# Reordering the second half of an input projection: two reused weight groups first, compression under the convolution groups

## The chip, the cores and the metric

The kernel runs on one core of one Trainium2 chip. The metric is the device time of one launch in microseconds (us), lower is better.

## What is computed

One decoder layer on x of 2048 tokens by 1024 channels. The input projection gives 2328 columns: queries of 8 heads, three key/value pairs of 2 groups (compressed, selected, window), gates, and the input of a gated depthwise convolution over time of 512 channels and 31 taps. Then come sparse attention in blocks of 128 queries, a layer norm and SiLU over the convolution, an output projection over both, and a feed-forward network.

```
xn = rms_norm(x); proj = xn @ w_in                      # 1024 -> 2328
q, kc_raw, vc_raw, ks, vs, kw, vw, gates, conv_in = split(proj)
k_cmp, v_cmp = compress(kc_raw), compress(vc_raw)       # silu(blocks of 32 tokens @ w1) @ w2
o_nsa  = g0*softmax(q k_cmp) v_cmp + g1*softmax(q k_sel) v_sel + g2*softmax(q k_win) v_win
o_conv = silu(layer_norm(depthwise_conv(a * sigmoid(gate))))
x = x + concat(rms_norm(o_nsa), rms_norm(o_conv)) @ w_out
y = x + (silu(h @ w_gate) * (h @ w_up)) @ w_down,  h = rms_norm(x)
```

## The kernel before, in words

Every product of full precision is three matmuls of halves: weights and activations are split in a high and a low float16 part, and `mm3` (L244) issues high by high, high by low and low by high.

**Phase A** (`phase_A_body`, L360) is the input projection, in two halves of 1024 tokens, s = 0 and s = 1. A half has two blocks of 512 tokens, h = 0 and 1. The 1024 rows of w_in are used in nine column parts: parts 0 to 3 are the convolution's (a channel block and its gate, 256 columns), part 4 the raw compressed keys and values (`kcvc`), parts 5 to 8 the row groups, whose result has tokens on partitions: part 5 at column 768 of the kept row (values and gates), 6 at column 0, 7 at 256, 8 at 512. The list `seq` (L416) names the order in which parts are loaded (`loads`), normed (only for s = 0) and split (`casts`: ScalarE rounds the high half, L466, VectorE makes the low half, L467). The split weights wh and wl have 3 buffers each.

- A convolution part (`conv`, L476) is four products of 24 matmuls of 512 columns (`colmm`); ScalarE puts tanh of the gate into `sg` (one buffer) and the channel into `hc`, VectorE multiplies them (L488).
- The depthwise filter of a channel block is 50 VectorE steps on 512-wide tiles (`filters`, L318 to L353, with the running sums ev, fq and od), called taps. They are put into a list, and `mm3` takes one from it each time 2232 matmul columns have been issued (`PACE`, L50). What is left at the end of a half is issued there in one go (`while self.taps`, L601).
- `conv_tail` (L610) finishes 128 tokens of the convolution: four transposes on TensorE, then layer norm and SiLU in five VectorE and four ScalarE instructions, and a store to DRAM (`mixc`). The tile z has 2 buffers, the tile zt one. The eight tails of s = 0 are called during the first convolution part of s = 1. The eight tails of s = 1 come in phase B, at a priority a little under the attention's.
- A row step (`rows`, L507) is 24 matmuls for 128 tokens, a copy by ScalarE and a store.

In s = 1 a generator `ahead()` is pumped between the products: first `compress` (L639), 16 chunks of weights that ScalarE and POOL split (L235, L236) and of blocks that POOL splits too (L665), with 12 matmuls each; then `early_B` (L761), which prepares the first two query blocks: `prep0` and `prep0q` (rms norm, rope and transposes of q), `value_scales` (L740; the largest value is spread over the partitions by two small TensorE steps, L191 and L196, with a VectorE reduction between them, L193), and `prep1` (L944 to L983, the compressed attention of the block). In the kernel before, the pump gives two steps at each break of convolution parts 2 and 3 and one for each row step.

**Phase B** goes over 16 query blocks: `attend` (L1066 on: scores L1084 to L1089, exponentials L1094, value products L1117), and `project` (L1184 on: the output projection of two blocks' tokens, with its weights split at L242 and L243 before the first). The pool that holds the project's tiles (and the closing tile `zo` of each attention block, L1172) lies in the memory of phase A's long-lived pool, so the first of them waits until the last conv tail is done. Then the feed-forward network runs from about 1430 us on.

**The order.** Within phase A, TensorE's instructions stand as they are written (a manual schedule, L533). All other engines, and TensorE in phase B, get their order from a list scheduler by priorities; taps have a priority 3000 lower than the rest. Each engine runs its instructions in the order so fixed.

Of the kernel before, what the change touches and what calls it, by code (L numbers as in the profile page):

```python
# [94 lines left out]
class Body:  # L95
    def __init__(self, tc, I, out, phases="ABC"):
        self.tc, self.nc, self.I, self.out = tc, tc.nc, I, out
        with ExitStack() as ctx:
            self.c = ctx.enter_context(tc.tile_pool(name="const", bufs=1))
            self.dr = ctx.enter_context(tc.tile_pool(name="dram", bufs=1, space=DRAM))  # L100
            self.taps, self.credit = [], 0
            self.consts()
            pb = ctx.enter_context(ExitStack())
            with ExitStack() as pa:
                self.sa = pa.enter_context(tc.tile_pool(name="sbA1", bufs=1, side="right"))
                tails = self.phase_A(pb)
                self.open_B(pb)
                with tc.high_priority(-TAILP):
                    for t in tails:
                        self.conv_tail(*t)  # L110
            pc = ctx.enter_context(ExitStack())
            self.open_project(pc)
            last = self.phase_B()
            pb.close()
            self.ffn(last, pc.close)
            self.end()
# [243 lines left out]
    def phase_A_body(self, pb, ctx, ctx0):  # L360
# [52 lines left out]
                  ([(768, 896), (1024, 1152)], 512)]  # L413
        parts = [[(1816 + j * 128, 1944 + j * 128), (1304 + j * 128, 1432 + j * 128)] for j in range(4)]
        parts += [[(512, 768)]] + [g[0] for g in groups]
        seq = [(s, at) for s in range(2) for at in (0, 1, 4, 2, 3, 5, 6, 7, 8)]  # L416
        raws, sums, cast = [], [], []

        def loads(to):
# [50 lines left out]
        def take(t):  # L470
            loads(t + 2)
            norms(t + 1)
            casts(t)
            return cast[t]

        def conv(j, x2, w2, between):  # L476
            hc = sa.tile([128, 2, 512 + HALF], F32, name="hc", tag="hc", bufs=HCB)
            nc.vector.tensor_copy(hc[:, :, :HALF], halo[:, j])
            for h in range(2):
                p = colmm(0, x2[h], w2)  # L480
                between(2 * h)
                t = s0.tile([128, 2, 256], F32, name="sg", tag="sg", bufs=1)
                nc.scalar.activation(t, p.rearrange("p (m e) -> p e m", e=2), AF.Tanh, scale=w2[3])
                p = colmm(128, x2[h], w2)
                between(2 * h + 1)
                hv = hc[:, :, HALF + h * 256:HALF + (h + 1) * 256]
                nc.scalar.activation(hv, p.rearrange("p (m e) -> p e m", e=2), AF.Copy, scale=w2[2])
                nc.vector.scalar_tensor_tensor(hv, t, 1.0, hv, op0=ALU.add, op1=ALU.mult)  # L488
            nc.vector.tensor_copy(halo[:, j], hc[:, :, 512:])
            acc = sa.tile([128, 1024], F32, name="acc", tag="acc", bufs=4)  # L490
            self.taps += self.filters(hc, acc, j)
            return acc
# [40 lines left out]
        with tc.manual_schedule(engines={mybir.EngineType.PE}):  # L533
# [6 lines left out]
            for s in range(2):  # L540
# [10 lines left out]
                accs = []  # L551
                nxt = ahead() if s else iter(())
                pump = lambda: next(nxt, None)
                for j in range(4):
                    at = 9 * s + j + (j > 1)
                    w2 = take(at)

                    def between(i):
                        if i == 1:
                            casts(at + 1)  # L560
                        if j == 0 and i < 2:
                            step(st1, 4)
                        else:
                            for t in tails[:2 if j == 0 else 1]:
                                self.conv_tail(*tails.pop(0))
                            for _ in range(PUMP[j]):
                                pump()
                    accs.append(conv(j, x2, w2, between))
                    if j == 1:
                        next(gains, None)  # L570
                        kcvc(s, x2, take(at + 1), lambda: casts(at + 2))
                    if j == 2 and s == 0:
# [1 line left out]
                        next(out_scale)  # L574
                self.pace = PACE[2 * s + 1]
                for gi in range(2):
                    t = 9 * s + 5 + gi
                    wg = take(t), groups[gi][1]
                    for h in range(2):
                        rows(s, h, x2, wg, pump)  # L580
# [1 line left out]
                            casts(t + 1)  # L582
                        if s == 0 and gi == 1:
                            next(out_scale)
                norms(9 * s + 8)
                wg = [(take(9 * s + 5 + gi), groups[gi][1]) for gi in (2, 3)]
                for g in wg:
                    rows(s, 0, x2, g, pump)
                casts(9 * s + 9)
                if s == 0:  # L590
                    first, st0 = turn(load(1, 0))
                    rows(s, 1, x2, wg[0], lambda: step(st0, STEP0))
                    xs = load(1, 1)
                    rows(s, 1, x2, wg[1], nothing)
                    second, st1 = turn(xs)
                else:
                    for g in wg:
                        rows(s, 1, x2, g, pump)
                    for _ in nxt:
                        pass  # L600
                while self.taps:  # L601
# [158 lines left out]

    def early_B(self):  # L761
        self.sp = {c: self.prep0(c) for c in range(NE)}
        for _ in range(4):
            yield
        scales = self.value_scales()
        for _ in range(EW - 4):
            next(scales, None)
            yield
        for c in range(NE):
            self.prep0q(self.sp[c])  # L770
# [960 lines left out]
```

## Time and profile before

| what | value |
|---|---|
| median of 3 runs | 2785.3 us (2785.23 to 2785.98) |
| the profiled execution | 2789.21 us |
| its span in the profile | 2787.4 us, mean granted TensorE clock 0.958 |
| TensorE matmul, busy | 2495.3 us, 90% |
| VectorE, busy | 2182.1 us, 78% |
| ScalarE, busy | 1508.9 us, 54% |
| POOL, busy | 1319.8 us, 47% |
| second half of phase A | 244 to 554 us |
| phase B before the feed-forward network | 554 to about 1430 us |

Times inside the program count from the start of the span. An engine's idle time costs something only where another engine ends up waiting for it on the way to the end. The table is an average over the program: the feed-forward network, the last half, is nearly all TensorE, whereas in the stretch that the change touches VectorE and TensorE are about equally full.

### The profile page before, as it was taken

How to read it: one execution, taken by the hardware profiler on the slowest of the kernel's cores; microseconds unless marked ns; L12 is line 12 of the kernel's file. 1: busy time of each engine (PE TensorE's matmuls, PEld its weight loads, DVE VectorE, ACT ScalarE, POOL GpSimd, SP SyncE). 2: the span in 40 equal slices, each digit the busy share in tenths (PEclk: the TensorE clock that was granted, in tenths of full speed). 3: DMA queues.
4: the chain of work that ended last, by engine and by line, in shares of the span. 5: the costliest groups of instructions: out<-in, count | busy, mean ns of one | idle time of the engine just before them, and what ended most of it. 6: DMA issues, size and time to landing. Idle time of an engine off the chain costs nothing. (4 is left out here: it accounts for less than half of the span.)

```text
span 2787.4 us, 46922 instructions
## 1 busy us (share of the span) xinstructions
PE 2495.3 (90%) x17430; PEld 1522.7 (55%) x17430; DVE 2182.1 (78%) x3463; ACT 1508.9 (54%) x3153; POOL 1319.8 (47%) x1117
## 2 busy tenths in 40 slices
PE   6997977867889998889986999998899999899999
PEld 3485446745667777777873444443344444344444
DVE  4898898889999899889666766668766765797995
ACT  7534633477666666555564555555455444445543
POOL 1101345254444444334455665667666664951850
PEclk9998988878999999999997999999999999999999
DMA  6133212113211111000015433443344332677343
GB/s 216 55 111 104 85 52 63 56 48 114 74 57 42 45 47 36 28 28 28 28 43 187 139 105 105 133 136 113 118 136 136 116 100 106 212 243 260 105 148 110
DMA packets 254781, 283.33 MB, mean 102 GB/s; under 512 B 20304, under 2 KB 174344, under 8 KB 254552
## 3 DMA queue, kind: packets, MB, share of 16 engines
q1 hardware_dynamic: 253904, 278.93, 31.2%
q8 instruction: 136, 2.23, 0.3%
q0 software_dynamic: 400, 1.31, 0.1%
q14 instruction: 93, 0.76, 0.1%
q10 hardware_dynamic: 248, 0.09, 0.0%
HBM read 201.96 MB, written 78.32 MB: 101 GB/s over the span
## 5 line engine op out<-in xcount | busy, mean ns | idle before, releaser
L1394 PE MATMUL ps<-oph,wh 128*128 128x512 f16 x1232 | 470.8, 382 | 30.1 <-DVE u L1472 12.7
L1397 PE MATMUL ps<-opl,wh 128*128 128x512 f16 x1232 | 470.1, 382 | 2.8 <-POOL opl L1353 1.3
L1396 PE MATMUL ps<-oph,wl 128*128 128x512 f16 x1232 | 470.6, 382 | 1.3 <-DVE wl L1387 1.3
L1104 POOL TENSOR_TENSOR mpl<-mp 128x512 f16<-128x512 f32 x206 | 232.0, 1129 | 238.2 <-ACT mp L1094 218.7
L1094 ACT ACTIVATE mp<-s,few 128x512 f32<-128x512 f32 x412 | 271.3, 688 | 100.6 <-PE s L1086 70.7
L1041 DVE TENSOR_REDUCE bx<-pp 128x8 f32<-128x512 f32 (+1 forms) x426 | 274.7, 664 | 29.8 <-PE pp L1037 27.5
L1605 PE MATMUL acc<-wl,ah 128*128 128x512 f16 x604 | 229.8, 380 | 20.4 <-DVE wl L1557 20.4
L1604 PE MATMUL acc<-wh,ah 128*128 128x512 f16 x604 | 229.8, 380 | 5.1 <-ACT wh L1556 5.1
L1606 PE MATMUL acc<-wh,al 128*128 128x512 f16 x604 | 229.9, 381 | 0.0
L1396 PEld LDWEIGHTS <-wl 128*128 128x128 f16 x1232 | 121.1, 98 | 179.2 <-issue 35.2
L1084 PE MATMUL s<-r,k 128*128 128x256 f16 x824 | 209.2, 275 | 10.6 <-ACT mp L1094 10.2
L1086 PE MATMUL s<-r,k 100*128 100x256 f16 x824 | 210.1, 276 | 0.0
L1386 ACT ACTIVATE wh<-sm,wsc 128x512 f16<-128x512 f32 x176 | 125.8, 715 | 148.3 <-PE ps L1396 146.4
L1117 PE MATMUL uu<-v,mp 128*128 128x129 f16 x1648 | 203.9, 224 | 2.4 <-ACT us L1140 2.4
L1394 PEld LDWEIGHTS <-wh 128*128 128x128 f16 x1232 | 122.1, 99 | 152.6 <-issue 5.5
L1387 DVE SCALAR_TENSOR_TENSOR wl<-sm,wsc,wh 128x512 f16<-128x512 f32 x176 | 183.4, 1043 | 26.1 <-ACT wh L1386 26.1
L1397 PEld LDWEIGHTS <-wh 128*128 128x128 f16 x1232 | 121.3, 98 | 147.2 <-issue 3.9
L1117 PE MATMUL uu<-v,mpl 128*128 128x65 f16 x1648 | 188.1, 196 | 10.8 <-DVE mpl L1104 8.5
L1556 ACT ACTIVATE ah<-ar,sac 128x512 f16<-128x512 f32 x151 | 108.6, 719 | 162.6 <-PE acc L1605 157.3
L1387 DVE SCALAR_TENSOR_TENSOR wl<-wr,wsc,wh 128x512 f16<-128x512 f32 x132 | 141.8, 1075 | 69.5 <-ACT wh L1386 68.1
L1557 DVE SCALAR_TENSOR_TENSOR al<-ar,sac,ah 128x512 f16<-128x512 f32 x151 | 160.4, 1062 | 45.6 <-ACT ah L1556 45.5
L1104 DVE TENSOR_TENSOR mpl<-mp 128x512 f16<-128x512 f32 x206 | 165.6, 811 | 30.8 <-ACT mp L1094 30.2
(382 smaller groups left out, 6942.2 us busy)
## 6 DMA issues: line engine op xcount, KB each, us to landing
wr<-in_w_gate_up_dram SPq DMA_DIRECT2D x88, 512.0 KB, 3.8
ar<-S SPq DMA_DIRECT2D x88, 256.0 KB, 3.1
S<-at SPq DMA_DIRECT2D x85, 256.0 KB, 2.0
wf<-in_w_down_dram SPq DMA_DIRECT2D x85, 256.0 KB, 4.8
A<-at SPq DMA_DIRECT2D x64, 256.0 KB, 2.1
ar<-A SPq DMA_DIRECT2D x63, 256.0 KB, 2.9
raw<-in_w_in_dram SPq DMA_DIRECT2D x44, 256.0 KB, 3.8
wr<-in_w_down_dram SPq DMA_DIRECT2D x22, 512.0 KB, 3.6
```

The lines of the kernel that those rows point to most:

```text
L1041: nc.vector.tensor_reduce(bx[:, h0:h0 + per, 2 * (ka - k0):2 * (kb - k0)], mp.rearrange("p h (b x) -> p h b x", x=64), axis=AX.X, op=ALU.max)
L1086: nc.tensor.matmul(s[:, i], self.k2[br][:KAUG, g, ks], r2[:KAUG, h0:h0 + 2, :], start=False, stop=base is None, skip_group_check=True)
L1094: nc.scalar.activation(p32[:, :n], s[:, :n], AF.Exp, scale=self.kap[:, job[0][0]:job[0][0] + 1])
L1104: eng.tensor_tensor(pl[:, :n], p32[:, :n], ph[:, :n], op=ALU.subtract)
L1117: nc.tensor.matmul(uu[:, hh, :n], w[:, i, hh, :], self.v[br][:, self.slot(br, kt), g, :n], start=new, stop=last and n == 129, skip_group_c ...
L1387: nc.vector.scalar_tensor_tensor(lo, x, sw, hi, op0=ALU.mult, op1=ALU.subtract)
L1394: nc.tensor.matmul(p, wh[:, k, :], xh[:, k, :], start=start and k == 0, stop=False, skip_group_check=True)
L1396: nc.tensor.matmul(p, wl[:, k, :], xh[:, k, :], start=False, stop=False, skip_group_check=True)
L1397: nc.tensor.matmul(p, wh[:, k, :], xl[:, k, :], start=False, stop=stop and k == 3, skip_group_check=True)
L1604: nc.tensor.matmul(p[i], ah[:, ts], wh, start=s, stop=False, skip_group_check=True)
L1605: nc.tensor.matmul(p[i], ah[:, ts], wl, start=False, stop=False, skip_group_check=True)
L1606: nc.tensor.matmul(p[i], al[:, ts], wh, start=False, stop=stop and k == NH2 - 1, skip_group_check=True)
```

## The change

For s = 1 the order of parts is new. The two row groups that s = 0 did last (parts 7 and 8) come first, with the split weights that s = 0 left in SBUF, so that `seq` has 16 entries instead of 18 and those two weight loads and splits disappear. The eight row steps of the block h = 0 each carry one step of the second block's transposes, the eight of h = 1 one conv tail of s = 0. Then comes `kcvc`, then the convolution parts 0 to 3, with two pump steps at each break but the very first, and last the row groups 5 and 6. `value_scales` waits for row group 5 by a flag (`vready`), and `prep1` is drained after the last row step. The tile `sg` moves to another pool. In lines of the changed kernel, code behind L602 is 6 lines later and code behind L780 8 lines later than before.

```diff
-        seq = [(s, at) for s in range(2) for at in (0, 1, 4, 2, 3, 5, 6, 7, 8)]
+        seq = [(0, at) for at in (0, 1, 4, 2, 3, 5, 6, 7, 8)] + [(1, at) for at in (4, 0, 1, 2, 3, 5, 6)]
...
-                t = s0.tile([128, 2, 256], F32, name="sg", tag="sg", bufs=1)
+                t = sb.tile([128, 2, 256], F32, name="sg", tag="sg", bufs=1)
...
+                if s:
+                    def tail():
+                        if tails:
+                            self.conv_tail(*tails.pop(0))
+                    for g in wg:
+                        rows(s, 0, x2, g, lambda: step(st1))
+                    for g in wg:
+                        rows(s, 1, x2, g, tail)
+                    kcvc(s, x2, take(9), lambda: casts(10))
                 for j in range(4):
-                    at = 9 * s + j + (j > 1)
+                    at = 10 + j if s else j + (j > 1)
...
-                        if j == 0 and i < 2:
+                        if s == 0 and j == 0 and i < 2:
                             step(st1, 4)
-                        else:
-                            for t in tails[:2 if j == 0 else 1]:
-                                self.conv_tail(*tails.pop(0))
-                            for _ in range(PUMP[j]):
+                        if s and j + i:
+                            for _ in range(PUMP[max(j, 2)]):
                                 pump()
                     accs.append(conv(j, x2, w2, between))
-                    if j == 1:
+                    if j == 1 and s == 0:
...
                 for gi in range(2):
-                    t = 9 * s + 5 + gi
+                    t = (14 if s else 5) + gi
...
-                norms(9 * s + 8)
-                wg = [(take(9 * s + 5 + gi), groups[gi][1]) for gi in (2, 3)]
-                for g in wg:
-                    rows(s, 0, x2, g, pump)
-                casts(9 * s + 9)
+                    self.vready = s and gi == 0 or self.vready
                 if s == 0:
+                    norms(8)
+                    wg = [(take(5 + gi), groups[gi][1]) for gi in (2, 3)]
+                    for g in wg:
+                        rows(s, 0, x2, g, pump)
+                    casts(9)
...
                 else:
-                    for g in wg:
-                        rows(s, 1, x2, g, pump)
                     for _ in nxt:
                         pass
...
-        for _ in range(4):
+        yield
+        while not self.vready:
             yield
         scales = self.value_scales()
-        for _ in range(EW - 4):
-            next(scales, None)
+        for i in range(7):
+            if i < 2 or i > 4:
+                next(scales, None)
             yield
```

How this moves instructions shows at three places. The first is VectorE around the reduction of the value scales (L193). Before, it stands behind two steps of the query preparation (L880, L884):

```order
L348 SCALAR_TENSOR_TENSOR od<-fx,wsum,od 128x512
L880 TENSOR_TENSOR qn<-big,qn 128x8x64
L884 TENSOR_TENSOR kl<-big,kn 128x256
L193 TENSOR_REDUCE vsc<-pp 3x1
L872 TENSOR_TENSOR big<-big,rp 128x12x32 x2
```

In the changed kernel, with the reduction that it needs (L751) and taps around it:

```order
L348 SCALAR_TENSOR_TENSOR acc<-fx,wsum,od 128x512
L751 TENSOR_REDUCE vmx<-vmax 128x2
L336 SCALAR_TENSOR_TENSOR ev<-hc,wdw,ev 128x512
L351 TENSOR_TENSOR fx<-hc 128x527
L336 SCALAR_TENSOR_TENSOR ev<-hc,wdw,ev 128x512
L193 TENSOR_REDUCE vsc<-pp 3x1
```

The reduction no longer has query preparation ahead of it; on TensorE 96 matmuls stand between L191 and L196 instead of 24.

The second place is VectorE at the conv tails of s = 1 (st, mv and z are their tiles). Before, they stand between steps of the attention (bx, mm, qn, mxc):

```order
L618 BN_STATS st<-z 128x6
L1050 TENSOR_REDUCE mm<-bx 128x8
L618 BN_STATS st<-z 128x6
L1052 SCALAR_TENSOR_TENSOR mm<-mm,lns 128x16
L620 BN_AGGR mv<-st 128x2 x2
L1055 CAST qn<-mm 128x8 x2
L628 SCALAR_TENSOR_TENSOR z<-z,mv,lng 128x512
L1056 TENSOR_TENSOR qn<-mm,qn 128x8 x2
```

In the changed kernel the last taps (od, acc) stand ahead of them, and nothing between the tails:

```order
L347 SCALAR_TENSOR_TENSOR od<-fx,wsum,fp 128x512
L936 SCALAR_TENSOR_TENSOR v_5435<-rv,vsc,v_5435 128x2x64
L348 SCALAR_TENSOR_TENSOR od<-fx,wsum,od 128x512 x14
L348 SCALAR_TENSOR_TENSOR acc<-fx,wsum,od 128x512
L624 BN_STATS st<-z 128x6
L626 BN_AGGR mv<-st 128x2
L634 SCALAR_TENSOR_TENSOR z<-z,mv,lng 128x512
L624 BN_STATS st<-z 128x6
```

Of the 200 taps of s = 1, 67 stand behind the last row step of phase A: 40 spread over the attention and 27 ahead of the tails. Before, all 200 stand inside phase A. The 40 VectorE instructions of the eight tails follow one another without any other, and the first split of the output weights (L243) comes after the last of them.

The third place is TensorE at the same tails (x is the tile of their transposes, o the first attention block's output). Before, in phase B:

```order
L917 LDWEIGHTS kl
L917 MATMUL pp<-id_65,kl 128x128
L614 MATMUL x<-id_60,acc 128x128 x7
L1084 LDWEIGHTS k_5453
L1084 MATMUL s<-r_4994,k_5453 128x256
L614 MATMUL x<-id_60,acc 128x128
```

In the changed kernel:

```order
L991 LDWEIGHTS ph
L991 MATMUL pp<-vc,ph 128x96
L620 MATMUL x<-id_60,acc 128x128 x30
L1203 MATMUL x<-id_60,o 128x128 x4
L1069 LDWEIGHTS qn
```

Thirty of the 32 transposes follow one another, and the first `project` comes directly behind them. Ahead of this place stand 40 exponentials (L1094 of before), as many as before finishes in its first 195 us of phase B, but no `project`, of which before has done two by then (64 matmuls for each of the three lines of `mm3`).

## Rows read from the trace of the kernel before

**Rows 1.** Busy time of each engine by stretches; the first line names the columns.

```profile
core 0: us, PE busy (x) PEld busy (x) DVE busy (x) ACT busy (x) POOL busy (x), PEclk, DMA share, GB/s
244.00:554.00 310.00, 252.91 (x1655) 172.22 (x1654) 275.25 (x394) 133.92 (x365) 111.30 (x96) 0.89 0.22 67
525.00:554.00 29.00, 24.80 (x246) 21.10 (x245) 23.12 (x43) 12.31 (x43) 0.00 (x0) 0.88 0.09 29
554.00:749.00 195.00, 140.14 (x1264) 104.67 (x1260) 175.23 (x385) 141.97 (x435) 95.06 (x107) 0.82 0.25 81
749.00:1080.00 331.00, 296.35 (x3299) 242.11 (x3298) 303.46 (x677) 212.27 (x585) 151.43 (x157) 0.98 0.14 45
```

**Rows 2.** Waits of TensorE's matmuls from 244 to 554 us: total, times, longest.

```profile
PE pp L196 <- DVE vsc L193: 18.7, 1, 18.7
PE mm L687 <- issue: 11.1, 1, 11.1
PE x L614 <- DVE acc L348: 5.0, 1, 5.0
PE mm L687 <- DVE cs L681: 4.7, 3, 4.1
PE mm L252 <- DVE xtl L282: 4.3, 1, 4.3
```

**Rows 3.** Timeline of TensorE behind that wait at L687: start, duration.

```profile
394.76 0.63 PE L251 MATMUL mm<-xth,wh 128*128 128x512 f16 x1
...
398.88 0.38 PE L252 MATMUL mm<-xtl,wh 128*128 128x512 f16 x1
399.09 0.38 PE L253 MATMUL mm<-xth,wl 128*128 128x512 f16 x1
```

**Rows 4.** Timeline of VectorE, at the value scales' reduction.

```profile
489.93 1.07 DVE L880 TENSOR_TENSOR qn<-big,qn 128x512 f16<-128x512 f32 x1 [3.90 <-ACT qn L879]
490.92 0.94 DVE L884 TENSOR_TENSOR kl<-big,kn 128x256 f16<-128x256 f32 x1
491.79 0.27 DVE L193 TENSOR_REDUCE vsc<-pp 3x1 f32<-3x128 f32 x1
```

**Rows 5.** Timeline of VectorE, taps: beside POOL's work, and in chains alone.

```profile
350.23 1.79 DVE L336 SCALAR_TENSOR_TENSOR ev<-hc,wdw,ev 128x512 f32<-128x512 f32 x1
351.94 1.78 DVE L348 SCALAR_TENSOR_TENSOR od<-fx,wsum,od 128x512 f32<-128x512 f32 x1
...
358.36 0.74 DVE L336 SCALAR_TENSOR_TENSOR ev<-hc,wdw,ev 128x512 f32<-128x512 f32 x1
...
505.37 9.29 DVE L336 SCALAR_TENSOR_TENSOR ev<-hc,wdw,ev 128x512 f32<-128x512 f32 x11
```

**Rows 6.** Timeline of POOL at the same time, compression.

```profile
351.44 1.74 POOL L665 TENSOR_TENSOR cxl<-cxf,cxh 128x512 fp32r<-128x512 f32 x1
353.14 1.73 POOL L236 TENSOR_TENSOR wcl<-cxf,wch 128x512 fp32r<-128x512 f32 x1
```

**Rows 7.** VectorE's groups by line, 554 to 749 us: count, busy, mean ns.

```profile
L243 DVE SCALAR_TENSOR_TENSOR wol<-raw,wos,woh 128x1024 f16<-128x1024 f32 x8 | 10.2, 1270 | 0.3 <-ACT woh L242 0.2
L628 DVE SCALAR_TENSOR_TENSOR z<-z,mv,lng 128x512 f32<-128x512 f32 x8 | 7.5, 933 | 0.0
L629 DVE SCALAR_TENSOR_TENSOR z<-z,rs,lnb 128x512 f32<-128x512 f32 x8 | 7.0, 870 | 1.5 <-POOL rs L219 1.4
...
L632 DVE SCALAR_TENSOR_TENSOR z<-zt,z 128x512 f32<-128x512 f32 x8 | 5.8, 729 | 1.9 <-ACT zt L631 1.9
...
L618 DVE BATCH_NORM_STATS2 st<-z 128x6 f32<-128x512 f32 x8 | 5.5, 685 | 0.2 <-ACT z L616 0.2
...
L1203 DVE TENSOR_TENSOR mtl<-x,mth 128x512 f16<-128x512 f32 x6 | 4.1, 681 | 0.7 <-ACT mth L1197 0.7
L1215 DVE SCALAR_TENSOR_TENSOR h<-x,few,h 128x256 f32<-128x256 f32 x8 | 3.8, 473 | 0.4 <-PE x L253 0.4
```

**Rows 8.** Timeline of ScalarE: one pair of conv tails of s = 0.

```profile
277.50 0.60 ACT L616 ACTIVATE z<-x 128x512 f32<-128x512 f32 x1 [5.45 <-PE x L614]
278.36 0.60 ACT L616 ACTIVATE z<-x 128x512 f32<-128x512 f32 x1 [0.26 <-PE x L614]
...
287.12 0.72 ACT L636 ACTIVATE z<-z,ss 128x512 f32<-128x512 f32 x1 [0.37 <-POOL ss L219]
```

**Rows 9.** Timeline of ScalarE: the last conv tail, then the first `zo`.

```profile
636.22 0.72 ACT L636 ACTIVATE z<-z,ss 128x512 f32<-128x512 f32 x1 [0.71 <-POOL ss L219]
...
640.46 0.62 ACT L1172 ACTIVATE zo<-o 128x512 f32<-128x512 f32 x1
```

**Rows 10.** ScalarE's and TensorE's groups by line, 554 to 749 us.

```profile
L1094 ACT ACTIVATE mp<-s,few 128x512 f32<-128x512 f32 x40 | 26.5, 689 | 2.2 <-PE s L1089 1.7 <-PE uu L1117 0.4
...
L251 PE MATMUL x<-woh,mth 128*128 128x256 f16 x65 | 19.3, 297 | 9.0 <-DVE h L1215 7.3 <-DVE mtl L1203 0.9 <-ACT woh L242 0.8
```

More of the change, by code (lines that the diff above doesn't have):

```diff
@@ L100, in __init__ @@
             self.dr = ctx.enter_context(tc.tile_pool(name="dram", bufs=1, space=DRAM))
-            self.taps, self.credit = [], 0
+            self.taps, self.credit, self.vready = [], 0, False
             self.consts()
```

## The prediction

> **What bounds the kernel now.** I read the busy time by stretches first. In the second half of phase A, 310 us, TensorE is busy for 252.9 us and VectorE for 275.3; from 554 to 749 us VectorE is busy for 175.2 of 195 us and TensorE for 140.1; from 749 to 1080 us both are nearly full, 296.4 and 303.5 of 331 us [rows 1]. So the first stretch offers 57 us of TensorE's waits, and a lag handed on to the third is hardly caught up, since VectorE rests there for 27.5 us and TensorE for 34.6. The waits come next: 18.7 us for the value scales' reduction, 11.1 and 4.7 at the compression's second product, 5.0 for the last tap of s = 0 before its tails and 4.3 for the second block's transposes [rows 2]. Then the timelines, for the price of a tap, a tail and a slow matmul.
>
> **The change, part by part.**
>
> *Two loads and splits less.* Four low halves go from VectorE. The same shape costs 1.27 us elsewhere [rows 7], so 5 us. No wait in the list names these splits, so they give TensorE nothing directly; four ScalarE casts and six DMA issues on SP's queue go too, at nothing, since ScalarE is busy for 134 of 310 us and no wait is put down to a weight DMA.
>
> *Row groups first.* The waits at the start of s = 1 (4.3 and 5.0 us) lie where TensorE has nothing else ahead of tails and transposes. In the new order sixteen row steps with weights already there lie around them, so I take both at zero: −9.3 us.
>
> *Value scales.* The reduction waited in VectorE's queue behind L880 and L884, which waited for ScalarE and that for POOL [rows 4]. In the new order no query preparation stands ahead of it, and 96 matmuls cover it: −18.7 us. The new wait on the flag holds back pump steps alone: it puts nothing into an engine's queue, and only the scales, `prep0q` and `prep1` come later. On SP's queue sixteen row stores move ahead and eight tail stores behind them; nothing in phase A reads either, so both at zero.
>
> *Compression under the convolution groups.* Its two long waits (11.1 + 4.7 us) sat where the second product of a chain was issued with nothing between. Now more lies between, but a filter competes on VectorE as before. I take half: −7.9 us; bounds 0 and −15.8.
>
> *Slow matmuls.* After the 11.1 us wait ten matmuls started in 4.1 us, at 0.41 us each, before the next took 0.21 [rows 3]: a wait of this kind costs 2 us more. The Trainium skill says the same of pauses ("TensorE: Matmul & The Clock Gate", section "HAM oscillation — how this bites in real kernels": short compute between waits starts cold each time). Three waits removed: −6 us.
>
> *prep1 loses its cover.* The two blocks' compressed attention runs from 525 to 554 us, in 29.0 us, with TensorE busy for 24.8 [rows 1]. Six row steps lay inside: 24 matmuls of 256 columns at half the 0.21 us of a 512-column one [rows 3], or 2.5 us each; with their gaps 2.8, so 16.7 us. These rows now run earlier and the chain of reductions, exponentials and transposes stands by itself: 12.3 us if the rows only filled time on top of the chain, 29 if it runs no faster without them. As taps still stand between its steps on VectorE I take 25.
>
> Sum: 310 − 9.3 − 18.7 − 7.9 − 6 = 268; the rows leave the end (−29.0 + 16.7) and the chain stands there (+25): 281 us. Phase A would end near **525 us**, 29 us earlier; with the chain at its bounds 512 to 529, and up to 540 where compression and taps meet worse.
>
> *Filters spill into phase B.* A tap is issued for each 2232 columns, and only while there is one. Now 16 row steps (24 × 256 columns each) and `kcvc` (4 × 24 × 512) run before a filter of s = 1 exists: 98,304 + 49,152 columns that carried 66 taps. That is the count of taps, 67, that stand behind the last row step; before, all stood inside phase A. A tap costs 0.67 us of pitch where it alternates with other work and 0.84 (9.29 over 11) in its own chain [rows 5]. Forty lie between attention steps: 27 to 34 us of VectorE, I take 27. The other 27, nearly one chain, stand together: 18 to 23 us, part of it beside TensorE's last attention work; 10 to 21, I take 16.
>
> *Attention before the tails.* From 554 to 749 us VectorE works 175.2 us. The tails are in this with 7.5 + 7.0 + 5.8 + 5.5 + 1.3 (the aggregations, unshown) = 27 us, and what the new order puts behind the tails with 10.2 for the output weights, 4.1 and 3.8 for the projection [rows 7] and some 3 of small ones, 21 us. Left are 127 us and the 27 of taps: 154 us at the least; with the 20 us for which VectorE waits now, 174. I take 170: to 695 us.
>
> *The tails as one block.* All tails now stand alone in VectorE's and ScalarE's queues, and 30 of their 32 transposes in TensorE's, with the first projection directly behind. What is queued behind the waiting transpose is everything: `project`, the next scores, the next products. z has two buffers, so tails go in pairs, and an undisturbed pair took 277.50 to 287.84, 10.3 us [rows 8]. Four pairs: 41 us, in which TensorE does 32 transposes and VectorE 27 us of work. Before, tails lay between attention steps, where VectorE worked 90% of the time, and cost little but their own 27 us. Nor can `project` come in between: its tiles wait for the last tail, as now, where the last z is scaled at 636.22 and the first `zo` follows at 640.46 [rows 9]. The block ends near 695 + 16 + 41 = 752 us.
>
> *What is still owed.* At that point 40 exponentials are done. Before has 40 by 749 us, and also two projections: 64 matmuls on each of three lines [rows 10], some 21 us at 0.107, and VectorE's 21 us above. In the following stretch VectorE is 92% and TensorE 90% busy [rows 1], so 21 us cost between 5 (taken from VectorE's rest) and 23 (21/0.92). I take 22, since both engines are full.
>
> Sum: 752 − 749 + 22 = **+25 us**. The phase A gain of 29 us is given back by about 43 us of taps, 14 us of the tails' block over the work in it, and the projections' being late. The profiled execution took 2789.2 us (span 2787.4 and 1.8 around it), 3.9 over the median of the runs; against the median 2785.3 the forecast is 2810.
>
> **A rule that speaks for the change.** While POOL's subtractions of the compression run (1.73 us each), taps take 1.78 us instead of 0.74, and the two take turns [rows 5, 6]. In the new order the first chunks of the compression fall into convolution part 0, where no tap of s = 1 exists yet; two POOL instructions for each of about five chunks give 10 slowed taps fewer, 10 us of VectorE. I leave them out of the sum, since VectorE has room in phase A once taps are spilled. The Trainium skill ("SBUF — State Buffer", section "Who interferes with whom") calls it an exclusive lock between a VectorE instruction with two SBUF inputs and a GpSimd instruction that reads SBUF; by that rule alone the taps lose 10 us and the time is 2800.
>
> **The rivals.**
>
> 1. *Absorbed, faster.* prep1's chain at its 12 us bound ends phase A at 512; VectorE never waits in the attention before the block (154: to 666); chain and pairs overlap with TensorE's backlog (10 + 35: to 711); 22 owed. That is 711 − 749 + 22 = −16: 2769 us. It decides on VectorE's waits before the tails: under 5 us of 154 instead of 20 of 195. For: VectorE's list holds the 40 taps, which wait for no other engine. Against: the tails, which did the same before, are gone from there. Chance 0.14.
> 2. *Hidden, no change.* TensorE has 55 us of rest between 554 and 749 us anyway; if the block of tails only gathers these, and half of the owed work goes into rests later, then 752 − 749 − 10 + 10 = about 0, 2780 to 2792: 0.14.
> 3. *Phase A does not gain.* Filters stay VectorE's backlog: if all 32 of POOL's subtractions slow two taps each by 1.04 us, that is 67 us of VectorE, where before some 26 taps (27 us, in the pattern of [rows 5]) were slowed; a difference of 40, and `sg`, with one buffer, holds the next product until VectorE has multiplied. Half of it would come through to TensorE: phase A ends at 545, and the rest stands as before: 25 + 20 = +45, 2830 us. For: VectorE is at 89% in phase A [rows 1]. Chance 0.14.
> 4. *The tails' block is longer*, 60 us, as the mixc store must land before z is free again, and ScalarE's order keeps the next scores waiting: +40, 2825 us, in the same direction; part of the forecast's range.
>
> **How the numbers follow.** A difference of 0.2%, 5.6 us, is about what a measurement of this kernel tells from none. Forecast with rival 4: 0.58, 2792 to 2830. Rival 1: 0.14, 2755 to 2780. Rival 2: 0.14, of which half lies within 0.2% and the rest evenly to both sides. Rival 3: 0.14, 2820 to 2850. Faster 0.14 + 0.04 = 0.18, same 0.07 + 0.02 from the forecast's edge = 0.09, slower 0.73. The range for 8 in 10 takes in the forecast, rival 2 and the near halves of rivals 1 and 3: 2772 to 2838.
>
> **What would show it.** Right: phase A's last row step near 505 and prep1 without rows to 525; no wait at L196 above 2 us; taps (L348) up to 710 us; a stretch of about 40 us with TensorE under 20% busy, ScalarE and VectorE only in the tails' lines, and slow matmuls behind it; the first `zo` near 755 us instead of 640 [rows 9]; the feed-forward network starting 25 us later. Wrong: attention going on beside the tails; phase A ending after 540; or the first TensorE work of the feed-forward network earlier than before.

## The result, and the profile after

The changed kernel took **2863.9 us** (2862.2 to 2866.5), the kernel before 2785.3: a ratio of 1.0283, interval 1.0270 to 1.0297. It is 79 us slower. The forecast was slower, at 2810 with a range up to 2838; the direction held and the size did not. The profiled execution has a span of 2860.6 us against 2787.4, so 73.2 us are to be found in the two traces.

Busy time by stretches, the changed kernel, columns as in [rows 1]:

```profile
244.00:554.00 310.00, 255.09 (x1689) 174.46 (x1688) 234.14 (x357) 140.96 (x393) 109.40 (x99) 0.89 0.21 63
525.00:554.00 29.00, 15.94 (x126) 11.23 (x126) 27.60 (x54) 16.92 (x59) 4.91 (x3) 0.56 0.08 21
554.00:749.00 195.00, 106.31 (x963) 77.69 (x962) 169.43 (x374) 103.12 (x344) 82.49 (x86) 0.72 0.07 21
749.00:1080.00 331.00, 268.71 (x2749) 215.60 (x2750) 265.19 (x570) 197.22 (x528) 130.58 (x142) 0.93 0.23 70
266.00:352.00 86.00, 80.81 (x514) 52.63 (x513) 37.90 (x52) 56.60 (x108) 33.66 (x45) 0.98 0.38 109
693.00:766.00 73.00, 8.76 (x30) 5.38 (x30) 47.92 (x93) 21.16 (x42) 18.78 (x33) 0.51 0.07 26
```

The same stretch from 266 to 352 us in the kernel before:

```profile
266.00:352.00 86.00, 75.97 (x350) 38.65 (x350) 76.64 (x111) 49.50 (x92) 28.24 (x38) 0.90 0.23 72
```

VectorE, the engine that the change was not about, is busy for 37.9 us of these 86 instead of 76.6. TensorE has its matmuls there and hardly waits; what is missing is a filter to run beside them. The first step of the first filter (L335) starts 64 us later than before; before, then after:

```profile
287.92 0.55 DVE L335 TENSOR_SCALAR ev<-hc,wdw,vec 128x512 f32<-128x512 f32 x1 [0.22 <-PE mm L253]
352.27 1.52 DVE L335 TENSOR_SCALAR ev<-hc,wdw,vec 128x512 f32<-128x512 f32 x1
```

Later, from 693 to 766 us, TensorE does 30 transposes in 73 us at a granted clock of 0.51.

Waits of TensorE's matmuls, the changed kernel, 244 to 900 us (total, times, longest):

```profile
PE x L620 <- ACT z L622: 28.8, 7, 9.2
PE x L620 <- DVE acc L348: 24.4, 2, 14.7
PE pp L191 <- DVE vmx L751: 17.4, 1, 17.4
PE x L1203 <- ACT o L1182: 15.8, 3, 13.2
```

The waits of [rows 2] are gone, the 18.7 us at L196 too, though in sum TensorE rests from 244 to 554 us nearly as long as before, 55 us instead of 57. One of 17.4 us stands at L191, one step earlier, for VectorE again. The three others are the block: the last taps, the eight tails one behind the other, and the first projection. Its timeline on TensorE:

```profile
692.71 0.21 PE L991 MATMUL pp<-vc,ph 128*128 128x96 f16 x1
702.66 0.48 PE L620 MATMUL x<-id,acc 128*128 128x128 f32 x1 [9.74 <-DVE acc L348]
717.82 0.47 PE L620 MATMUL x<-id,acc 128*128 128x128 f32 x1 [14.68 <-DVE acc L348]
...
729.22 1.12 PE L620 MATMUL x<-id,acc 128*128 128x128 f32 x4 [7.32 <-ACT z L622]
...
741.25 1.12 PE L620 MATMUL x<-id,acc 128*128 128x128 f32 x4 [8.68 <-ACT z L622]
...
753.76 1.11 PE L620 MATMUL x<-id,acc 128*128 128x128 f32 x4 [9.17 <-ACT z L622]
768.07 1.12 PE L1203 MATMUL x<-id,o 128*128 128x128 f32 x4 [13.19 <-ACT o L1182]
```

From 692.9 to 717.8 TensorE waits for left-over taps, from there to 768.1 for tails, which come in pairs. The first pair takes 10.3 us, as in [rows 8], the other three take 12.0 to 12.5. ScalarE's timeline:

```profile
718.33 0.60 ACT L622 ACTIVATE z<-x 128x512 f32<-128x512 f32 x1 [23.16 <-PE x L620]
...
724.91 0.63 ACT L637 ACTIVATE zt<-z 128x512 f32<-128x512 f32 x1 [0.54 <-DVE z L635]
725.53 0.72 ACT L642 ACTIVATE z<-z,ss 128x512 f32<-128x512 f32 x1
...
728.59 0.58 ACT L622 ACTIVATE z<-x 128x512 f32<-128x512 f32 x1
730.80 0.60 ACT L622 ACTIVATE z<-x 128x512 f32<-128x512 f32 x1 [1.64 <-DMA mixc<-z]
...
736.33 0.72 ACT L642 ACTIVATE z<-z,ss 128x512 f32<-128x512 f32 x1 [1.81 <-POOL ss L219]
736.95 0.61 ACT L637 ACTIVATE zt<-z 128x512 f32<-128x512 f32 x1
...
765.65 0.61 ACT L1180 ACTIVATE zo<-o 128x512 f32<-128x512 f32 x1
...
833.68 0.63 ACT L1180 ACTIVATE zo<-o 128x512 f32<-128x512 f32 x1 [0.39 <-DVE s L1007]
...
865.43 0.64 ACT L1180 ACTIVATE zo<-o 128x512 f32<-128x512 f32 x1
```

From the second pair on, the copy of a pair's second tail into z waits until the store of an older one has landed, since z has two buffers; by this it starts 2.2 us behind the first copy instead of 1.8. The rest is mostly ScalarE's order: the first tail's closing scale (L642), which waits for POOL, stands ahead of the second tail's first tanh (L637), which VectorE had made ready at 735.6; in the first pair it stands behind it. The closing `zo` comes at 765.6 instead of 640.5 [rows 9], the second at 833.7, the next ones 32 us apart, as attention blocks whose exponentials had been done before the block of tails are closed and projected.

To see where the 73 us arise I cut both traces where ScalarE starts the first, the 41st, the 121st and the 301st exponential (L1094 before, L1102 after), points of equal progress in the attention. Before:

```profile
244.00:574.70 330.70, 264.50 (x1735) 179.83 (x1734) 293.38 (x433) 148.14 (x402) 119.13 (x107) 0.88 0.22 68
574.70:767.50 192.80, 146.38 (x1367) 111.82 (x1366) 173.86 (x387) 137.45 (x439) 94.30 (x105) 0.85 0.24 79
767.50:955.50 188.00, 165.00 (x1800) 133.04 (x1800) 171.78 (x385) 122.35 (x336) 86.70 (x89) 0.97 0.16 50
955.50:1302.20 346.70, 312.98 (x3580) 258.31 (x3578) 308.84 (x662) 208.53 (x473) 140.99 (x149) 0.98 0.11 34
```

After:

```profile
244.00:561.40 317.40, 259.14 (x1712) 177.18 (x1711) 240.38 (x374) 145.79 (x420) 113.56 (x102) 0.88 0.22 64
561.40:777.90 216.50, 109.31 (x978) 79.94 (x977) 174.57 (x374) 111.85 (x339) 84.43 (x94) 0.70 0.10 29
777.90:1030.80 252.90, 216.95 (x2203) 173.91 (x2202) 207.91 (x448) 151.14 (x422) 99.24 (x104) 0.96 0.24 72
1030.80:1376.40 345.60, 311.86 (x3581) 257.73 (x3579) 309.33 (x663) 207.40 (x467) 141.24 (x149) 0.99 0.11 34
```

The last stretch is equal within about a microsecond: nothing to speak of is lost or won behind the 121st exponential. Ahead of it VectorE works 293.4 + 173.9 + 171.8 = 639 us before and 240.4 + 174.6 + 207.9 = 623 after, and rests 37 + 19 + 16 = 72 against 77 + 42 + 45 = 164. So the lag of 75 us at the 121st is 92 us more of VectorE's rest less 16 of its work: 40 of the rest in phase A, 23 around the block, 29 while projections are caught up. Counted by TensorE, the same lag is 8 us less of rest in phase A, 61 more around the block, 13 more behind it, and some 10 us more of busy time. The sums locate rests; which of them is a cause, only the runs below can tell.

The marks themselves say when the lag shows: the first exponential comes 13 us early, the 41st 10 us late, the 121st 75 us late. The stretch between the last two takes 253 us instead of 188, because more is left to do in it: at the 41st exponential the kernel before has closed three attention blocks and issued three projections, the changed one has closed one and projected none. TensorE's work up to there is 42 us less after (368.5 against 410.9), VectorE's 52 us less (415.0 against 467.2), of which 16 never come. While this is made up, TensorE is busy for 86% of the time, before for 88%.

### The profile page after: what moved, and what is told of

The parts are those of the page before. It is cut to its first block, busy times and chain, and to the rows that moved or that the text cites. A ratio compares the mean times of both kernels' runs of the same rounds, so it can differ in the third digit from the quotient of the medians.

```text
span 2860.6 us, 46892 instructions
## 1 busy us (share of the span) xinstructions
PE 2501.7 (87%) x17430; PEld 1526.8 (53%) x17430; DVE 2168.6 (76%) x3459; ACT 1507.0 (53%) x3149; POOL 1316.6 (46%) x1117
## 5 line engine op out<-in xcount | busy, mean ns | idle before, releaser
L1102 ACT ACTIVATE mp<-s,few 128x512 f32<-128x512 f32 x412 | 271.3, 689 | 123.5 <-PE s L1094 83.7
L1094 PE MATMUL s<-r,k 100*128 100x256 f16 x824 | 214.1, 281 | 0.5 <-ACT r L1071 0.5
```

The lines of the kernel that those rows point to most:

```text
L1094: nc.tensor.matmul(s[:, i], self.k2[br][:KAUG, g, ks], r2[:KAUG, h0:h0 + 2, :], start=False, stop=base is None, skip_group_check=True)
L1102: nc.scalar.activation(p32[:, :n], s[:, :n], AF.Exp, scale=self.kap[:, job[0][0]:job[0][0] + 1])
```

## The experiments

Two theories were open at first. Theory 1: left-over taps sit behind the attention in VectorE's order, the tails then form a block, and the projections behind it come late. Theory 2: the new order of phase A costs the time, and the block only shows where.

**Slow taps in the kernel before.**

```diff
-PACE = (2232, 2232, 2232, 2232)
+PACE = (2232, 2232, 2800, 2800)
```

> The kernel before with one number changed: in the second half of phase A a tap is taken for each 2800 columns instead of 2232, so that taps are left over when the row steps are done; the order of the products, the weight loads and the compression are those of before. Theory 1 (left-over taps come after the attention in VectorE's order, the conv tails then stand as one block, and the projection waits behind it): the tails come after 40 exponentials, TensorE stands nearly still for 60 to 85 us near 700 us, and the time is 2835 to 2870 us. Theory 2 (the new order of phase A costs the time, the block only shows where it is paid): 2785 to 2800 us, since 20 taps of 0.7 us are all that moves.

2832.9 us, a ratio of 1.0171 (1.0156 to 1.0186), 48 us slower with one number changed and no product moved; 2 us under what theory 1 gave, far above theory 2. Its trace has 15 taps behind the first exponential. Its stretches from the first to the 41st and on to the 121st exponential:

```profile
554.10:748.90 194.80, 107.23 (x981) 79.25 (x980) 155.48 (x350) 113.10 (x345) 88.02 (x94) 0.73 0.11 35
748.90:1002.60 253.70, 217.96 (x2198) 174.31 (x2197) 208.10 (x448) 151.17 (x422) 99.30 (x104) 0.95 0.24 72
```

The 41st comes 19 us earlier than before in spite of the block, the 121st 47 us later (so 66 us are lost between them, not the 62 that the expectation of the eleventh run takes). The lag shows behind the block, in a stretch as long as in the changed kernel, 254 us. The spill alone brings this about.

**Left-over taps first, in the changed kernel.**

```diff
-        with self.tc.high_priority(-LOWP):
+        with self.tc.high_priority(-LOWP if after is not None else TAILP):
             i = self.taps.pop(0)()
```

> The changed kernel with one edit: taps that are left at the end of phase A get a priority above the attention's (200 up) instead of 3000 below it. Theory 1: the tails lie between the first 11 exponentials as in the kernel before, the block is gone, and the time is 2785 to 2815 us, 67 taps by 0.7 us (47 us of VectorE ahead of the attention) less what TensorE's part of the attention covers. Theory 2: 2845 to 2865 us, the block's waits only spread out.

2813.0 us, 1.0095 (1.0074 to 1.0115). One priority gives back 51 of the 79 us: the block goes, and from the first to the 301st exponential the kernel takes 732 us, 5 more than before. It reaches that first exponential 20 us late, though, since VectorE now works off the left-over taps with TensorE waiting:

```profile
554.68 0.47 PE L620 MATMUL x<-id,acc 128*128 128x128 f32 x1 [30.71 <-DVE acc L348]
```

So theory 1 holds for the larger part, and some 28 us are left that the new order of phase A may have to answer for.

**The same, with the value scales' steps later.**

```diff
-            if i < 2 or i > 4:
+            if i in (0, 4, 6):
```

> As the run before it, and the value scales' two steps on TensorE are issued three row steps later after the flag (L191 after five pump steps instead of two, L196 after seven instead of six). If TensorE bounds the end of phase A, the wait of 17.4 us at L191 falls to some 9 us and the time is 6 to 9 us under that run's; if VectorE does, through its queue of taps, reductions and query preparation, the time is within 3 us of it.

2810.7 us, 1.0092 (1.0074 to 1.0109), 2 us from the run before it. The 17.3 us wait at L191 left the list of long waits, and the time stayed, as expected if VectorE sets it.

**More buffers for the tails, in the changed kernel.**

```diff
-        z = sb.tile([128, 512], F32, name="z", tag="z", bufs=2)
+        z = sb.tile([128, 512], F32, name="z", tag="z", bufs=4)
-        t = sb.tile([128, 512], F32, name="zt", tag="zt", bufs=1)
+        t = sb.tile([128, 512], F32, name="zt", tag="zt", bufs=2)
```

> The changed kernel with four buffers for the tails' tile z instead of two, and two for zt instead of one. Theory 1 (the block of tails lies on the path, and its length is the latency of pairs: 48 us for eight tails that have 27 us of VectorE work): the block shrinks to 30 to 38 us and the time falls by 10 to 18 us, to 2846 to 2854. If the block is not on the path: 2860 to 2866, no change.

2844.7 us, 1.0214 (1.0198 to 1.0229): 19 us less, a little more than expected. `zo` starts at 750.1 instead of 765.6. From the first tail's copy into z to `zo` it takes 34 us instead of 47. Not all of the 19 us is the block's, since the edit holds for the tails of s = 0 too and the first exponential comes some 4 us earlier. But the block's latency is on the path: the 41st exponential comes 19 us earlier, and the stretch to the 121st takes 252 us as it did (253).

**Value scales later, in the kernel before.** L196 is issued five pump steps after L191 instead of one (the expectation says six); five row steps lie between them.

```diff
-        for _ in range(EW - 4):
-            next(scales, None)
+        for i in range(EW - 4):
+            if i in (0, 1, 6):
+                next(scales, None)
```

> The kernel before with one edit: the last step of the value scales (L196) is issued six pump steps after L191 instead of one, so that six row steps lie between them. If the 18.7 us wait at L196 is time of the kernel (TensorE sets the pace of the end of phase A), the wait goes and the time falls by 8 to 16 us, to 2769 to 2777. If VectorE sets it (its taps fill the wait and come later else), the wait moves to other places and the time is 2780 to 2787.

2785.2 us, 0.9998 (0.9988 to 1.0008): nothing. The longest wait of the stretch was worth nothing. Its waits on TensorE now:

```profile
PE mm L687 <- issue: 11.1, 1, 11.1
PE pp L972 <- ACT e L956: 10.2, 1, 10.2
PE mm L251 <- ACT ev L519: 7.4, 3, 4.3
```

From 473 to 493 us TensorE is busy for 13.5 us instead of 1.3, VectorE for 11.5 as before (11.3). Of the 17.6 us at the last two lines, 3.7 stood at the first of them before; the rest is new.

**Taps in time, in the changed kernel.**

```diff
-PACE = (2232, 2232, 2232, 2232)
+PACE = (2232, 2232, 1500, 1500)
...
-        with self.tc.high_priority(-LOWP):
+        with self.tc.high_priority(-LOWP if self.pace == PACE[0] else 0):
```

> The changed kernel with taps of the second half taken for each 1500 columns instead of 2232, at the priority of other work instead of 3000 lower; none is behind the first attention step in VectorE's order, and the tails lie among the first 12 exponentials. If what the flush at high priority left (28 us over the kernel before) is VectorE work whose cover was lost at the start of the half, faster taps can win back the rests of VectorE behind 330 us only: 2790 to 2808 us. If it is the chain of prep1 and the wait at L191: as the flush, 2808 to 2818.

2792.3 us, 1.0028 (1.0017 to 1.0038), in the first window. Faster taps fill VectorE's rests behind 352 us; the 48 us ahead of that they can't, and it is busy there for 37.4 us, as in the changed kernel.

**Slow taps, but not starved, in the kernel before.**

```diff
-PACE = (2232, 2232, 2232, 2232)
+PACE = (2232, 2232, 2600, 2600)
...
-        with self.tc.high_priority(-LOWP):
+        with self.tc.high_priority(-LOWP if after is not None else -TAILP):
```

> The kernel before with taps for each 2600 columns in the second half, as a smaller dose of the slow taps, but left-over taps 200 under the attention's priority instead of 3000, so that they and the tails lie among the first 15 exponentials. If starving of the left-over taps is what the 48 us of the slow taps were, and not the spill itself: 2775 to 2792 us. If a spill costs as such: 2800 to 2830.

2795.9 us, 1.0040 (1.0025 to 1.0054), between the two expectations: a spill that is not starved costs some 11 us, not 48. The dose is smaller (2600, not 2800), so the two don't compare exactly; but in both traces 15 taps stand behind the first exponential.

**Row groups first alone.** The second run's edit, with `kcvc` behind convolution part 1 and the compression's pump as in the kernel before:

```diff
-                    kcvc(s, x2, take(9), lambda: casts(10))
...
-                        if s and j + i:
-                            for _ in range(PUMP[max(j, 2)]):
+                        if s:
+                            for _ in range(PUMP[j]):
...
-                    if j == 1 and s == 0:
+                    if j == 1:
```

> The flush kernel with the row groups first alone: kcvc stands behind convolution part 1 again and the compression is pumped in parts 2 and 3 and the row steps, as in the kernel before. If the 28 us are lost cover for taps, the columns of kcvc carry 22 taps again, 15 us of VectorE: 2793 to 2803. If they come from prep1 standing without rows or the wait at L191, the time is 2808 to 2820, since fewer row steps are left for the pump.

2805.9 us, 1.0075 (1.0056 to 1.0093), between the two windows: 7 us less than the second run, half of the 15 us expected for 22 taps. It supports lost cover weakly and would bear other readings.

**Convolution part 0 between the reused row groups,** with the second run's priority and taps for each 1900 columns (`seq` and the steps between the products follow).

```diff
-PACE = (2232, 2232, 2232, 2232)
+PACE = (2232, 2232, 1900, 1900)
...
                     for g in wg:
                         rows(s, 0, x2, g, lambda: step(st1))
-                    for g in wg:
-                        rows(s, 1, x2, g, tail)
-                    kcvc(s, x2, take(9), lambda: casts(10))
...
                     accs.append(conv(j, x2, w2, between))
+                    if s and j == 0:
+                        for g in wg:
+                            rows(s, 1, x2, g, tail)
+                        kcvc(s, x2, take(10), lambda: casts(11))
```

> The changed kernel with convolution part 0 between the two blocks' reused row groups: eight row steps of block 0 with the transposes, then part 0, then the eight row steps of block 1 with the tails, then kcvc; the compression from part 1 on. Taps for each 1900 columns in the second half, left-over ones 200 above the attention. The first filter step then comes near 290 us, as in the kernel before, instead of 352. If VectorE's rest in the first 110 us of the half (48 of the 86 us from 266 to 352) is what was left of the loss, VectorE is busy for 65 to 77 us of that stretch, and the time is 2772 to 2786 us: the kernel before less four weight splits (5 us of VectorE) and its two early waits (9 us). If the position of the filters doesn't matter: 2792 to 2800, as with taps in time.

2789.4 us, 1.0017 (1.0008 to 1.0026), between the two windows, 3 us above the lower. VectorE is busy for 58.0 us from 266 to 352, not 65 to 77: two waits for ScalarE's weight split and channel copy (9.9 and 12.2 us) stand ahead of its taps. The first filter step came at 294.9, as expected. With the taps at the priority of other work as well:

```diff
-        with self.tc.high_priority(-LOWP if after is not None else TAILP):
+        with self.tc.high_priority(-LOWP if self.pace == PACE[0] else 0):
```

> The same with the taps of the second half at the priority of other work instead of 3000 under it, so that a tap that is due stands ahead of query preparation. Within 5 us of the run before it, either way, if VectorE is the bound and its order of little weight; over 8 us lower if late taps still hold up the attention's start.

2802.6 us, 1.0065 (1.0051 to 1.0078), 13 us slower, outside both expectations. The first exponential comes at 572.9 us, in the ninth run at 574.8, so it is not the attention's start that the pressing taps delay; the loss arises behind it, and what they hold up there was not followed up.

**Projections late, in the kernel before.**

```diff
-TAILP = 200
+TAILP = 4000
```

> The kernel before with one number changed: the conv tails of s = 1 are 4000 under the attention's priority instead of 200. No tap is left over and phase A is untouched; the tails lie apart (before exponentials 0, 0, 3, 12, 12, 31, 40, 40 instead of all among the first 12), but the first closing zo comes after 40 exponentials as in the changed kernel. It parts the block of tails from the lateness of the projections. In the run with slow taps the 41st exponential came 19 us earlier than in the kernel before although the block lay ahead of it, and 62 us were lost from there to the 121st. If the block (TensorE's rest while eight tails run alone) is what costs, only its last two tails and the restart are left here, some 25 us against 84: the time is 2790 to 2812 us. If projections that come late are costly as such, because the following stretch is full, the loss is nearly that of the slow taps: 2820 to 2840.

2829.2 us, 1.0159 (1.0144 to 1.0173), 44 us slower: the second window. Phase A is as before and no tap is left over. From the first to the 41st and on to the 121st exponential, and from the 40th to the 41st alone:

```profile
571.10:741.90 170.80, 106.20 (x965) 78.26 (x964) 141.66 (x324) 109.22 (x338) 80.77 (x88) 0.74 0.12 39
741.90:996.30 254.40, 218.54 (x2202) 174.83 (x2201) 207.90 (x448) 151.03 (x421) 98.96 (x104) 0.95 0.23 72
696.50:741.90 45.40, 14.76 (x134) 10.73 (x131) 27.31 (x72) 19.40 (x44) 15.74 (x25) 0.62 0.18 61
```

The attention runs 26 us ahead at the 41st exponential, and 41 us behind at the 121st. The second stretch takes 254 us, as in the changed kernel (253), with slow taps (254) and with four buffers (252), against 188 before: whenever the first closing waits for 40 exponentials, the same stretch grows by 64 to 66 us. But the run does not part the lateness of the projections from the block cleanly. Its last tails still run nearly alone: from the 40th to the 41st exponential TensorE is busy for 14.8 of 45.4 us.

**Convolution part 0 first, then all reused row groups.** Against the ninth run:

```diff
-PACE = (2232, 2232, 1900, 1900)
+PACE = (2232, 2232, 2100, 2100)
...
-                    for g in wg:
-                        rows(s, 0, x2, g, lambda: step(st1))
...
-                        if s == 0 and j == 0 and i < 2:
+                        if j == 0 and i < 2:
...
                     if s and j == 0:
+                        for g in wg:
+                            rows(s, 0, x2, g, tail)
```

> The changed kernel with convolution part 0 at the start of the half as in the kernel before, then the sixteen row steps with reused weights and the tails, then kcvc and the rest; taps for each 2100 columns, left-over ones 200 above the attention. It keeps the saving (two loads, 5 us of VectorE) and gives VectorE its taps from 290 us on beside 147 thousand columns. If VectorE's rest was the remaining loss: 2768 to 2784 us. If the end of phase A is short of row steps to cover the last part's filter (16 instead of 32 behind convolution part 3, some 40 taps left over): 2786 to 2800.

2788.0 us, 1.0005 (0.9996 to 1.0014): no difference from the kernel before. It lies in the second window. VectorE is busy for 71.6 us from 266 to 352. The first exponential comes at 559.4, 15 us earlier than before, and the 41st at 767.3, as before: what phase A gains, the stretch behind it loses. Two weight loads and splits less bring nothing here that these runs can tell, though other edits stand beside them, and no version tried beats the kernel before.

The second, sixth, ninth and last runs together bear on the 28 us that starved taps do not explain: more taps, or an earlier filter, bring back all but 2 to 7 of them. That fits VectorE's rest at the start of the half, but each of these runs changes more than one thing, so it is supported and not shown.

## Why the prediction was wrong, point by point

The chain of events was right: spilled taps, the tails as one block, projections behind it. Two terms of the sum failed, the gain of phase A and, the larger, what is still owed behind the block.

- **Two splits less, taken at 5 us of VectorE.** They are gone; the last run, where other things change too, shows no saving that can be told from nothing.
- **The waits at the start (−9.3), at the value scales (−18.7), in the compression (−7.9), and slow matmuls behind them (−6).** This is the first step that failed. The waits did go, as forecast, but others took their place, and the longest of them was not the kernel's time. I read TensorE's waits as what bounds phase A, though the busy times already said VectorE: 275 of 310 us against 253 [rows 1]. The fifth run took the 18.7 us away alone and won nothing. The third, likewise, at L191. Nor did the granted clock of the stretch rise: 0.89 before and after.
- **prep1 without cover (25, bounds 12.3 to 29).** The row steps end near 519.7, 15 us later than forecast, and the first exponential comes at 561.4: phase A gained 13 us, not 29, by that mark. My text had the right warning, 66 taps that lose their columns, but I charged it only to phase B. It is VectorE's rest in phase A: 77 us instead of 37.
- **Attention before the tails, to 695 us.** It ended at 692.9, by two errors that cancel, so by luck: it began later and ran with fewer waits of VectorE than I took (near the bound of 154, not 170).
- **The tails as one block.** Mechanism and place were right. The taps ahead of it took 24.9 us, not 16 (bounds 10 to 21): nearly nothing of attention was left beside them. The tails took 48 us (717.8 to 765.6), not 41: I had taken all pairs from one that no store holds up and in whose ScalarE order the second tail's tanh comes first. Rival 4 named the store, at 60 us; the order weighs more. End 765.6 instead of 752.
- **What is still owed, taken at 22 (bounds 5 to 23).** The second step that failed, and the larger: 73.2 − (765.6 − 749) = 56.6 us. I counted two projections and 21 us of work by the 749 us mark, on two engines side by side. At equal progress, the 41st exponential, it is three projections, 42 us of TensorE, and 52 of VectorE, of which 36 still have to be done. In the stretch up to the 121st TensorE then works 52 us longer than before and rests 13 longer, VectorE works 36 and rests 29 longer: 65 us in all. So the term was mis-sized, and the picture of two nearly full engines is about right for TensorE (86% busy) and wrong for VectorE (82%, before 91%). Why VectorE rests was not shown; that a projection is a chain through single-buffered tiles (`mth`, `mtl`, `x`) is my guess from the 32 us between closings.
- **The rivals.** The faster one and the hidden one are excluded. The third named VectorE as the bound of phase A, which the fifth run supports, but for the wrong reason: in the stretch to the first exponential its work fell from 293 to 240 us, not least because fewer taps ran there. The fourth had the right direction and is too small: 2825 us against 2864.
- **The rule on the shared lock** (the Trainium skill, "SBUF — State Buffer", section "Who interferes with whom"). The trace agrees in direction: from 244 us on, 27 taps take over 1.2 us before and 20 after, 7 fewer where I had 10. That, 5 us of splits and six taps of s = 0 that were done before 244 us are about the 16 us that VectorE works less. It was not what decided.

Of the 79 us, then, one priority gives back 51 (starved taps, block, late projections). Faster taps at normal priority in its place end another 21 lower, and 7 are left. How the 51 divide between the block and the late projections stays open.

## What to carry to other kernels

A long wait in the trace is time only if the engine that waits is the one that sets the end: compare the stretch's busy times first, and ask whether the engine waited for was itself full. When work is moved ahead of the start of a paced side job, count the columns that no longer carry it. Work of lowest priority that just fits is itself starved once it no longer fits, and everything behind it waits, so look at what the leftovers hold up, such as memory that another stage is waiting for. And compare two traces at points of equal progress, and count them exactly: in the eleventh run 45 us lie between the 40th exponential and the 41st.

## What the runs showed that I had not expected

In the kernel before, one number in the pace of the taps (2232 to 2800) or in the priority of the tails (200 to 4000) costs 44 to 48 us: the tuned order lies next to a cliff. And TensorE's granted clock was 0.51 over the 73 us of the block, in which it was busy for 8.8 us (that is the lower of its two levels, 1.2 of 2.4 GHz). It stayed low for a little behind the block: 256-column matmuls started 0.21 us apart at 778 us and 0.11 from 780.2. Beside the block this costs little.
